# Other addresses and another order for some of the matmuls of a two-layer decoder trunk: Up weights shifted in 16-byte steps, tokens read backwards, two tiles taken in turn

## The chip, the cores and the metric

One NeuronCore of one Trainium2 chip runs the whole forward pass for one sequence of 256 tokens. The metric is device time in microseconds (us) of one execution. Within the core, TensorE (PE) multiplies matrices from the on-chip memory SBUF into the accumulators of PSUM; VectorE (DVE) and ScalarE (ACT) do everything that is elementwise; GpSimd (POOL) does little here; SyncE (SP) issues nearly all transfers from the chip's main memory. The engines run on their own and wait for each other by semaphores. In a row of the profile, L169 is line 169 of the kernel, and PEld is the loading of a matmul's stationary operand, which overlaps the matmul before.

## The reference

The model width is 1024, there are 16 heads of 64, and the inner width of the channel mixer is 2816. Cut to what matters:

```python
x = x + short_conv_mixer(rms_norm(x, a_norm[0]), ...)         # layer 0
x = x + conv_glu_ffn(rms_norm(x, f_norm[0]), ...)
k_blk, v_blk, k_mean = shared_kv(x, kv_norm, w_k, w_v)         # layer 1
x = x + moba_attention(rms_norm(x, b_norm[0]), ...)
x = x + conv_glu_ffn(rms_norm(x, f_norm[1]), ...)
return rms_norm(x, final_norm)

def conv_glu_ffn(h, w_up, conv_w, conv_b, w_down):
    u = causal_dwconv(h @ w_up, conv_w) + conv_b               # 1024 -> 2 x 2816
    g, v = jnp.split(u, 2, axis=-1)
    return (jax.nn.silu(g) * v) @ w_down                       # 2816 -> 1024
```

All of it is in float32.

## The kernel before

**Three products for one.** Each operand of a large matmul is split into a high part (rounded to the type fp32r) and a low part (what is left, in fp32r too). A product of two such numbers is taken as high x high + high x low + low x high, so one tile product is three matmuls into one accumulator. `mm3` (lines 168 to 171) issues them: line 169 is weight-high with x-high, line 170 weight-high with x-low, line 171 weight-low with x-high. In the profile the parts are called hiB and loB (1 MB units of weights, 2048 floats per partition), hiS and loS (512 KB units), xh and xl (normed activations), sh and sl (hidden activations), oh and ol (attention output).

**Units.** Weights come in units, each loaded by SP into one of three raw buffers, rounded by ACT into hi (line 91) and subtracted by DVE into lo (line 97). `Unit.buffer` makes the hi and lo tiles: 64 floats longer than the unit, of which the unit takes a slice that begins `at_byte` bytes in. Up units had `at_byte` 0, most units of V 128, the Down units of layer 1 192.

**The channel mixer.** `ffn` (line 517) runs twice, for layer 0 and layer 1, over 22 Up units. For unit i, `up_step` takes 8 slices k of the width and, for each, two tiles of 128 weight columns (one of the gate half, one of the value half): 8 x 2 x 3 = 48 matmuls, with a tile of 128 x 128 weights as the stationary operand and one row of 256 tokens of xh or xl as the moving one. Both tiles accumulate in one PSUM bank, each in its half. Then DVE and ACT do scale, convolution and gate (`conv`, `gate`; lines 525, 532, 397, 543, 549, 394), and the Down unit of three steps earlier follows on PE with 24 matmuls. In layer 0 (`down_bank`) the weights are stationary and the tokens move; in layer 1 (`token_bank`) the tokens are stationary and the weights move.

**Order.** The schedule is written by hand: the program text sets the order on each engine. Within `conv`, DVE splits the low part of the next B unit, and ACT then the high part of one after it; within `gate` the same is done for S units. The load of a raw buffer is issued on SP when the low part has been taken from the unit that held it.

**Addresses.** The allocator puts hiB0 at byte 42560 of a partition, loB0 at 51008, and the other hi and lo tiles of both sizes likewise at 64 bytes past a multiple of 128. The tiles of xh and xl begin 64 past a multiple of 128 too; their class `Rows` puts the eight rows of tokens (1024 bytes each) 1216 bytes in, that is at a multiple of 128, and a second copy of row 0, `again`, 128 bytes in, that is at 64 past a multiple of 128. Units 2 and 6 of each `ffn` use the copy for k = 0. `Heads` places the rows of oh and ol at several offsets: rows 0 and 3 are at 64 past a multiple of 128, the others at a multiple. So nearly all matmuls of the kernel have the moving operand at 0 and the stationary one at 64 modulo 128 bytes, or the reverse where tokens are stationary; a few have both at 64.

Of the kernel before, what the change touches and what calls it, by code (L numbers as in the profile page):

```python
# [19 lines left out]
KT = D // 128  # L20
NH = 16
FF = 2816
FJ = FF // 128
# [5 lines left out]
BIG = 2 * KT * 128  # L29
# [13 lines left out]
def yoco_kernel(ctx: ExitStack, tc: tile.TileContext, t: dict, out: bass.AP):  # L43
    nc = tc.nc
    V, A, G, PE = nc.vector, nc.scalar, nc.gpsimd, nc.tensor
# [56 lines left out]
    def hi(tag, part=0, parts=1):  # L102

        n = ptr[tag][0]
        if n < len(by_tag[tag]) and (by_tag[tag][n].prev is None or by_tag[tag][n].prev.used):
            by_tag[tag][n].split_hi(part, parts)
            ptr[tag][0] += part == parts - 1

    def lo(tag, part=0, parts=1):

        n = ptr[tag][1]
        if n < len(by_tag[tag]) and by_tag[tag][n].hi is not None:
            by_tag[tag][n].split_lo(part, parts)
            if part == parts - 1:
                ptr[tag][1] += 1
                if n + RAW_BUFS[tag] < len(by_tag[tag]):
                    by_tag[tag][n + RAW_BUFS[tag]].load()
# [6 lines left out]
            MO += [Unit(t["w_mo"][i], SMALL) for i in ((0, 1) if j == 3 else (j - 2,))]  # L124
    MO += [Unit(t["w_mo"][j], SMALL) for j in (KT - 2, KT - 1)]
    UP, DN = [None, None], [None, None]
    UP[0] = [Unit(t["w_up"][0, i], BIG) for i in range(FJ)]
    DN[0] = [Unit(t["w_dn"][0, i], SMALL) for i in range(FJ)]
    heads = [("v", 0), ("v", 1), ("v", 2)] + [("q", j) for j in range(KT)] + [("v", 3)]
    WH = {k: Unit(t["w_v" if k[0] == "v" else "w_qk"][k[1]], BIG, (0, 1), 128 if k[0] == "v" and k[1] else 0)  # L130
# [12 lines left out]
    first = const.tile([128, 1], F32, name="first")  # L143
# [20 lines left out]
    def par(c, k=0):  # L164
        return pk[:, c + k:c + k + 1]


    def mm3(o, wh, wl, xh, xl, start, stop):
        PE.matmul(o, wh, xh, start=start, stop=False, skip_group_check=True)  # L169
        PE.matmul(o, wh, xl, start=False, stop=False, skip_group_check=True)  # L170
        PE.matmul(o, wl, xh, start=False, stop=stop, skip_group_check=True)  # L171

    def up_step(u, o, xh, xl, m, ks=range(KT), first=0, again=False):

        assert u.lo is not None
        wh, wl = u.v(u.hi, m), u.v(u.lo, m)
        for k in ks:
            h, lw = (xh.again, xl.again) if again and k == 0 else (xh[:, k, :], xl[:, k, :])
            for i in range(m):
                mm3(o[:, i, :], wh[:, k, i, :], wl[:, k, i, :], h, lw,  # L180
                    start=(k == first and i == 0), stop=(k == KT - 1))
        u.used = ks[-1] == KT - 1

# [52 lines left out]
    def up_bank():  # L236
        return psum.tile([128, 2, S], F32, name="up", bufs=3)
# [36 lines left out]
    def parts_tiles():  # L274
        return Rows("xh"), Rows("xl")
# [28 lines left out]
    def boundary(acc, x, gain, order=same, again=True):  # L304

        xh, xl = parts_tiles()
        sq = square_tile()
        for q in range(5):
            if q < 4:
                V.tensor_add(x[:, 2 * q:2 * q + 2, :], acc[q], x[:, 2 * q:2 * q + 2, :])  # L310
                scaled_hi(x, gain, (2 * q, 2 * q + 1), xh, order)
            if q:
                scaled_lo(x, gain, (2 * q - 2, 2 * q - 1), xh, xl, order)
                squares(x, sq, q - 1)
        sum_squares(sq, 0)
        lo("B", 0, 2)
        if not again:
            lo("B", 1, 2)
        sum_squares(sq, 1, order)
        if again:  # L320
            lo("B", 1, 2)
            tile_0_again(xh, xl)
        return xh, xl, sq
# [72 lines left out]
    def tap(o, u, w, back):  # L396
        V.scalar_tensor_tensor(o[:, back:], u[:, :S - back], w, o[:, back:], op0=OP.mult, op1=OP.add)  # L397
# [6 lines left out]
    xh, xl = parts_tiles()  # L404
# [23 lines left out]
    def mixer_a(j, fill=None):  # L428

        w = [par(P_CONV, 3 * j + n) for n in range(3)]  # L430
        m = tmp.tile([128, 2, S], F32, name="u", bufs=2)
        V.tensor_mul(m[:, 1, :], mc[j][:, 0, :], rr[:, 1, :])
        V.tensor_mul(m[:, 0, :], mc[j][:, 1, :], m[:, 1, :])
        o = tmp.tile([128, 2, S], F32, name="cv", bufs=2)
        A.activation(o[:, 0, :], m[:, 0, :], AF.Identity, scale=w[2])
        hi("B")
        if fill:
            lo(fill)
        tap(o[:, 0, :], m[:, 0, :], w[1], 1)
        tap(o[:, 0, :], m[:, 0, :], w[0], 2)  # L440
        V.tensor_mul(o[:, 1, :], o[:, 0, :], rr[:, 0, :])
        return o[:, 1, :]
# [33 lines left out]
    for i in range(2):  # L476
        o = mixer_a(i, "B")
# [8 lines left out]
    o = mixer_a(3, "B")  # L486
# [7 lines left out]
    for j in range(4, KT):  # L494
        mc[j] = up_bank()
        up_step(MC[j], mc[j], xh, xl, 2)
        o = mixer_a(j, "S")
# [13 lines left out]
    xh, xl, sq = boundary(acc, xT, P_FN)  # L511
# [5 lines left out]
    def ffn(layer, xh, xl, sq, bank=down_bank, between=None):  # L517
        ub, hd, low = {}, {}, {}
        up, dn = UP[layer], DN[layer]

        def conv(j, last=False):
            c0 = 2 * FJ * layer + j
            cw = [[par(P_FCW, 3 * (c0 + half * FJ) + n) for n in range(3)] for half in range(2)]
            u = tmp.tile([128, 2, S], F32, name="u", bufs=2)
            V.tensor_mul(u, ub[j], rr[:, 0:1, :].to_broadcast([128, 2, S]))  # L525
            if j:
                low[j - 1]()
            if not last:
                lo("B")
            o = tmp.tile([128, 2, S], F32, name="cv", bufs=2)  # L530
            for half in range(2):
                A.activation(o[:, half, :], u[:, half, :], AF.Identity, scale=cw[half][2],  # L532
                             bias=par(P_FCB, c0 + half * FJ))
            hi("B")
            for back in (1, 2):
                for half in range(2):
                    tap(o[:, half, :], u[:, half, :], cw[half][2 - back], back)
            return o

        def gate(j, o, last=False):  # L540
            sl = tmp.tile([128, S], F32, name="sl", tag="sc", bufs=4)
            hi("S", 0, 1 + last)
            A.activation(sl, o[:, 0, :], AF.Silu)
            if last:
                hi("S", 1, 2)
            else:
                lo("S")
            hid = tmp.tile([128, S], F32, name="hid", tag="sc", bufs=4)
            V.tensor_mul(hid, sl, o[:, 1, :])  # L549
            hd[j], zh, low[j] = split_act(hid, S, 64 if layer == 0 else 128)  # L550
            zh()
            if last:
                lo("S", 0, 2)
                low[j]()
                lo("S", 1, 2)

        acc = None
        for i in range(FJ):
            if i != 2:
                ub[i] = up_bank()  # L560
            if i == 1:
                n = 4 if layer else 3
                up_step(up[1], ub[1], xh, xl, 2, range(1, n), first=1)
                _, dg = rstd_cols(sq)
                lo("S")
                A.activation(first, ones[:, 0:1], AF.Silu)
                up_step(up[1], ub[1], xh, xl, 2, (*range(n, 7), 0, 7), first=1, again=True)
                n = 2 if layer else 1
                ub[2] = up_bank()
                up_step(up[2], ub[2], xh, xl, 2, range(1, n + 1), first=1)  # L570
                rr = rstd_rows(dg)
                gate(0, conv(0))
            else:
                again = i in (2, 6)
                ks = (*range(n + 1 if i == 2 else 1, 7), 0, 7) if again else range(8)
                up_step(up[i], ub[i], xh, xl, 2, ks, first=int(again), again=again)
            last = i == FJ - 1
            if i:
                o = conv(i, last)
                if not last:  # L580
                    gate(i, o)
            if between and 5 <= i < 21:
                between(i - 5)
            if i >= LAG:
                if i == LAG:
                    acc = [acc_bank() for _ in range(4)]
                    if bank is token_bank:
                        acc.append(psum.tile([128, 2, S], F32, name="misc", bufs=1))
                down_step(dn[i - LAG], acc, hd[i - LAG], first=(i == LAG), bank=bank)
            if last:  # L590
                gate(i, o, True)
            elif i == FJ - 2:
                hi("S")
                lo("S")
            if i == 0:
                hi("B")
        if bank is token_bank:
            token_last(dn[FJ - 3:], acc, [hd[j] for j in range(FJ - 3, FJ)])
        else:
            down_step(dn[FJ - 3], acc, hd[FJ - 3])  # L600
            down_last(dn[FJ - 2:], acc, [hd[FJ - 2], hd[FJ - 1]])
        return acc
# [293 lines left out]
    xh, xl, sq = boundary(acc, xT, P_FN + KT)  # L896
# [19 lines left out]
    w = tmp.tile([128, 16], F32, name="nl", bufs=1)  # L916
# [101 lines left out]
```

## Time and profile before

| | |
|---|---|
| time, median of 2 runs | 568.63 us (568.47 to 568.80) |
| span of the profiled execution, first to last instruction | 566.6 us |
| PE busy, share of the span, matmuls | 558.4 us, 99%, 4908 |
| DVE busy | 472.9 us, 83% |
| ACT busy | 341.7 us, 60% |
| DMA share of 16 engines, main queue | 52.9% |
| mean granted TensorE clock | 0.997 |

The profiled execution has a span of 566.6 us; the median of the runs is 2.0 us more, and that difference lies around the span (start and end of the execution), where the profile shows no instruction of the engines.

How to read it: a matmul's time in a row (276 ns) is that of one from start to end, but they are pipelined, and the next starts long before the first ends. So the pace of PE is read from windows: the length of a stretch divided by the matmuls that start in it. In a row of the view by windows, the number behind "x" counts every instruction that touches the stretch, so also the two or three that began before it.

### The profile page before, as it was taken

To read this page: it belongs to the slowest core of one execution; us is meant where nothing else is said; L and a number is where in the kernel's file an instruction comes from. 1 tells how busy PE (TensorE), PEld (TensorE's weight loads), DVE (VectorE), ACT (ScalarE), POOL (GpSimd) and SP (SyncE) were. 2 spreads that over 40 slices of the span, in tenths; PEclk is the share of its full clock that TensorE was granted. 3 is DMA by queue.
4 is the path that set the end of the run, shared out by engine and by line. 5 is a ranking of instruction groups with operands and counts; after the bars stand their busy time and mean duration, and the time that the engine had idled before them with its cause. 6 is when DMAs were issued, how large, how long until landed. Compare 5 with 4: busy or idle time off the path is not lost.

```text
span 566.6 us, 11823 instructions
## 1 busy us (share of the span) xinstructions
PE 558.4 (99%) x4908; PEld 554.1 (98%) x4908; DVE 472.9 (83%) x817; ACT 341.7 (60%) x525; POOL 10.4 (2%) x32
## 2 busy tenths in 40 slices
PE   8999999999999999999999999999999999999995
PEld 8999999999999999999999999999999999999995
DVE  5998869899877787787897999858999888889876
ACT  7765437567654665466756777656676556546534
POOL 0400000000000000000000000000000000000001
PEclk9999999999999999999999999999999999999998
DMA  8986583447556545655265565644656554563211
GB/s 294 387 300 220 181 299 120 149 152 243 193 197 224 186 160 213 223 175 197 75 214 168 202 206 216 195 178 150 223 186 223 223 193 159 208 222 117 72 38 75
DMA packets 24181, 108.48 MB, mean 191 GB/s; under 512 B 2736, under 2 KB 5440, under 8 KB 16192
## 3 DMA queue, kind: packets, MB, share of 16 engines
q1 hardware_dynamic: 23840, 107.43, 52.9%
q8 instruction: 38, 0.62, 0.4%
q10 hardware_dynamic: 288, 0.30, 0.1%
q14 instruction: 15, 0.12, 0.1%
HBM read 106.65 MB, written 1.07 MB: 190 GB/s over the span
## 4 chain that ended last, share of the span: by engine, by line
PE 97%; DMA 1%; ACT 1%; issue 0%; DVE 0%; SPq 0%; POOLq 0%; POOL 0%; ACTq 0%
PE up L171 20%; PE up L169 20%; PE up L170 20%; PE acc L169 7%; PE acc L171 7%; PE acc L170 7%; PE acc L203 3%; PE acc L200 3%; PE acc L202 3%; PE up L757 1%; PE acc L627 1%; PE acc L629 1%; PE acc L630 1%; DMA xres<-xT 1%; PE acc L682 1%; PE misc L203 0%
## 5 line engine op out<-in xcount | busy, mean ns | idle before, releaser
L169 PE MATMUL up<-xh,hiB 128*128 128x256 f32 x944 | 261.4, 277 | 0.8 <-ACT hiB L91 0.8
L171 PE MATMUL up<-xh,loB 128*128 128x256 f32 x944 | 261.1, 277 | 0.3 <-DVE loB L97 0.2
L170 PE MATMUL up<-xl,hiB 128*128 128x256 f32 x944 | 260.8, 276 | 0.0
L169 PEld LDWEIGHTS up<-xh,hiB 128*128 128x128 f32 x944 | 177.2, 188 | 1.5 <-ACT hiB L91 1.0
L171 PEld LDWEIGHTS up<-xh,loB 128*128 128x128 f32 x944 | 177.2, 188 | 0.7 <-DVE loB L97 0.7
L170 PEld LDWEIGHTS up<-xl,hiB 128*128 128x128 f32 x944 | 177.3, 188 | 0.0
L97 DVE TENSOR_TENSOR loB<-rawB,hiB 128x2048 fp32r<-128x2048 f32 (+2 forms) x76 | 147.8, 1948 | 3.7 <-ACT hiB L91 3.5
L91 ACT ACTIVATE hiB<-rawB 128x2048 fp32r<-128x2048 f32 (+1 forms) x73 | 123.6, 1697 | 15.2 <-PE up L170 7.0
L532 ACT ACTIVATE cv<-u,pk 128x256 f32<-128x256 f32 x88 | 48.2, 595 | 69.3 <-DVE u L525 69.3
L97 DVE TENSOR_TENSOR loS<-rawS,hiS 128x1024 fp32r<-128x1024 f32 (+2 forms) x73 | 83.5, 1147 | 6.4 <-ACT hiS L91 6.0
L397 DVE SCALAR_TENSOR_TENSOR cv<-u,pk,cv 128x255 f32<-128x255 f32 x192 | 81.4, 479 | 2.7 <-ACT cv L532 1.7
L91 ACT ACTIVATE hiS<-rawS 128x1024 fp32r<-128x1024 f32 (+2 forms) x73 | 72.0, 987 | 8.9 <-PE acc L170 5.3
L525 DVE TENSOR_TENSOR u<-up,rr 128x512 f32<-128x512 f32 x44 | 30.3, 688 | 44.9 <-PE up L171 43.0
L171 PE MATMUL acc<-sh,loS 128*128 128x256 f32 x240 | 66.2, 276 | 0.0
L169 PE MATMUL acc<-sh,hiS 128*128 128x256 f32 x240 | 66.2, 276 | 0.0
L170 PE MATMUL acc<-sl,hiS 128*128 128x256 f32 x240 | 66.2, 276 | 0.0
L394 ACT ACTIVATE sh<-hid 128x256 fp32r<-128x256 f32 x52 | 21.7, 417 | 58.5 <-DVE hid L549 53.7
L171 PEld LDWEIGHTS acc<-sh,loS 128*128 128x128 f32 x240 | 45.1, 188 | 0.0
L169 PEld LDWEIGHTS acc<-sh,hiS 128*128 128x128 f32 x240 | 45.1, 188 | 0.0
L170 PEld LDWEIGHTS acc<-sl,hiS 128*128 128x128 f32 x240 | 45.0, 188 | 0.0
L200 PE MATMUL acc<-hiS,sh 128*128 128x256 f32 x154 | 42.5, 276 | 0.0
L202 PE MATMUL acc<-loS,sh 128*128 128x256 f32 x154 | 42.5, 276 | 0.0
(180 smaller groups left out, 780.3 us busy)
## 6 DMA issues: line engine op xcount, KB each, us to landing
rawB<-w_up SPq DMA_DIRECT2D x44, 1024.0 KB, 4.7
rawS<-w_dn SPq DMA_DIRECT2D x44, 512.0 KB, 3.4
rawB<-w_qk SPq DMA_DIRECT2D x8, 1024.0 KB, 4.8
rawB<-w_mc SPq DMA_DIRECT2D x6, 1024.0 KB, 8.1
rawS<-w_mo SPq DMA_DIRECT2D x8, 512.0 KB, 5.1
rawB<-w_v SPq DMA_DIRECT2D x4, 1024.0 KB, 4.7
rawS<-w_o SPq DMA_DIRECT2D x8, 512.0 KB, 4.0
rawS<-w_mb SPq DMA_DIRECT2D x7, 512.0 KB, 5.7
```

Of the source, the lines that this page charges most:

```text
L91: A.activation(self.hi[:, c], self.raw[:, c], AF.Copy)
L97: V.tensor_sub(self.lo[:, c], self.raw[:, c], f32(self.hi[:, c]))
L169: PE.matmul(o, wh, xh, start=start, stop=False, skip_group_check=True)
L170: PE.matmul(o, wh, xl, start=False, stop=False, skip_group_check=True)
L171: PE.matmul(o, wl, xh, start=False, stop=stop, skip_group_check=True)
L200: PE.matmul(o, hh[:, tok], u.hi[:, f], start=(first and (apart or d.start == 0)), stop=False, skip_group_check=True)
L202: PE.matmul(o, hh[:, tok], u.lo[:, f], start=False, stop=False, skip_group_check=True)
L203: PE.matmul(o, hl[:, tok], u.hi[:, f], start=False, stop=last, skip_group_check=True)
L394: return (h, lw), lambda: A.activation(h, src, AF.Copy), lambda: V.tensor_sub(lw, src, f32(h))
L397: V.scalar_tensor_tensor(o[:, back:], u[:, :S - back], w, o[:, back:], op0=OP.mult, op1=OP.add)
L525: V.tensor_mul(u, ub[j], rr[:, 0:1, :].to_broadcast([128, 2, S]))
L532: A.activation(o[:, half, :], u[:, half, :], AF.Identity, scale=cw[half][2], bias=par(P_FCB, c0 + half * FJ))
```

## The change

Three edits, all of which touch only matmuls of the two `ffn` calls and the buffers they read:

1. **Offsets.** Up unit i of layer 0 gets `at_byte` = 16 x max(0, i - 5) modulo 256: units 0 to 5 and 21 stay at 0, unit 6 gets 16, unit 7 gets 32, and so on to unit 20 with 240. ACT and DVE write the parts there, and PE loads its stationary tiles from there.
2. **Backwards.** In layer 1, units 9, 13, 17 and 21 pass `rev` to `up_step`. The row of 256 tokens is then read from its last to its first element, and the accumulator is written from its last to its first element as well, so each result lands where it did.
3. **In turn.** In layer 1, units 7, 11, 15 and 19 take their two tiles in turn: for each k, high x high of tile 0 and of tile 1, then high x low of both, then low x high of both.

The third edit moves instructions on PE. Below is the start of unit 7 of layer 1 as the program before has it; misc is the last accumulator of the Down unit ahead of it, hiB1_5410 and loB1_5505 are the two parts of the unit's weights, up_5659 its PSUM bank.

```order
L202 MATMUL misc_5326<-loS1_5420,sh_5319 128x256
L203 MATMUL misc_5326<-hiS1_5417,sl_5320 128x256
L169 MATMUL up_5659<-xh_4952,hiB1_5410 128x256 [waits PE_49]
L170 MATMUL up_5659<-xl_4953,hiB1_5410 128x256
L171 MATMUL up_5659<-xh_4952,loB1_5505 128x256 [waits DVE_49]
L169 MATMUL up_5659<-xh_4952,hiB1_5410 128x256
```

And the same place in the changed program, where line 182 issues the matmuls of such a unit:

```order
L208 MATMUL misc_5326<-loS1_5420,sh_5319 128x256
L209 MATMUL misc_5326<-hiS1_5417,sl_5320 128x256
L182 MATMUL up_5659<-xh_4952,hiB1_5410 128x256 [waits PE_49]
L182 MATMUL up_5659<-xh_4952,hiB1_5410 128x256
L182 MATMUL up_5659<-xl_4953,hiB1_5410 128x256 x2
L182 MATMUL up_5659<-xh_4952,loB1_5505 128x256 [waits DVE_49]
L182 MATMUL up_5659<-xh_4952,loB1_5505 128x256
L182 MATMUL up_5659<-xh_4952,hiB1_5410 128x256 x2
```

The first matmul that needs the low part, and so waits for DVE, is now the fifth of the unit and no longer the third. The end of the same unit before, with the Down unit behind it:

```order
L170 MATMUL up_5659<-xl_4953,hiB1_5410 128x256
L171 MATMUL up_5659<-xh_4952,loB1_5505 128x256
L200 MATMUL acc_5322<-hiS2_5519,sh_5426 128x256 [waits Activation_49]
L202 MATMUL acc_5322<-loS2_5522,sh_5426 128x256 [waits DVE_49]
L203 MATMUL acc_5322<-hiS2_5519,sl_5427 128x256
```

And after:

```order
L182 MATMUL up_5659<-xl_4953,hiB1_5410 128x256 x2
L182 MATMUL up_5659<-xh_4952,loB1_5505 128x256 x2
L206 MATMUL acc_5322<-hiS2_5519,sh_5426 128x256 [waits Activation_49]
L208 MATMUL acc_5322<-loS2_5522,sh_5426 128x256 [waits DVE_49]
L209 MATMUL acc_5322<-hiS2_5519,sl_5427 128x256
```

The unit still ends with the low part, and nothing else has moved; DVE, ACT, POOL and SP have the same rows in the same order throughout. The first two edits leave every row in its place and change addresses and steps alone. The diff:

```diff
-    UP[0] = [Unit(t["w_up"][0, i], BIG) for i in range(FJ)]
+    UP[0] = [Unit(t["w_up"][0, i], BIG, at=16 * max(0, i - 5) % 256) for i in range(FJ)]
...
-    def up_step(u, o, xh, xl, m, ks=range(KT), first=0, again=False):
+    def up_step(u, o, xh, xl, m, ks=range(KT), first=0, again=False, order=lambda a: a, turns=False):
 
         assert u.lo is not None
         wh, wl = u.v(u.hi, m), u.v(u.lo, m)
         for k in ks:
             h, lw = (xh.again, xl.again) if again and k == 0 else (xh[:, k, :], xl[:, k, :])
+            if turns:
+                for n, (w, x) in enumerate(((wh, h), (wh, lw), (wl, h))):
+                    for i in range(m):
+                        PE.matmul(o[:, i, :], w[:, k, i, :], x, start=(k == first and n == 0 and i == 0),
+                                  stop=(k == KT - 1 and n == 2), skip_group_check=True)
+                continue
             for i in range(m):
-                mm3(o[:, i, :], wh[:, k, i, :], wl[:, k, i, :], h, lw,
+                mm3(order(o[:, i, :]), wh[:, k, i, :], wl[:, k, i, :], order(h), order(lw),
                     start=(k == first and i == 0), stop=(k == KT - 1))
...
-                up_step(up[i], ub[i], xh, xl, 2, ks, first=int(again), again=again)
+                up_step(up[i], ub[i], xh, xl, 2, ks, first=int(again), again=again,
+                        order=rev if layer and i > 6 and i % 4 == 1 else same,
+                        turns=layer and i > 6 and i % 4 == 3)
```

`rev` is `a[..., ::-1]`, `same` returns its argument.

## The prediction

> **What bounds the kernel now.** I read the page first: the busy times and the chain of work that ended last.
>
> ```profile
> PE 558.4 (99%) x4908; PEld 554.1 (98%) x4908; DVE 472.9 (83%) x817; ACT 341.7 (60%) x525; POOL 10.4 (2%) x32
> PE 97%; DMA 1%; ACT 1%; issue 0%; DVE 0%; SPq 0%; POOLq 0%; POOL 0%; ACTq 0%
> ```
>
> PE is the chain: 97% of the way from the end back to the start is matmul after matmul. Next, the view of waits for PE alone, because a PE that is busy 99% could still be held up a little at each unit.
>
> ```profile
> PE misc L142 <- POOL ones L138: 1.0, 1, 1.0
> PE up L169 <- ACT hiB L91: 0.8, 1, 0.8
> PE up L171 <- DVE loB L97: 0.2, 1, 0.2
> ```
>
> That is the whole list: 2.0 us of waiting in 566.6. No transfer, no split and no gate holds PE. So only the pace of the matmuls can move the time, and the third view is the one by windows: the length of a stretch against the matmuls that the program starts in it.
>
> ```profile
> core 0: us, PE busy (x) PEld busy (x) DVE busy (x) ACT busy (x) POOL busy (x), PEclk, DMA share, GB/s
> 141.81:264.21 122.40, 122.40 (x1082) 122.40 (x1081) 94.44 (x136) 70.22 (x91) 0.00 (x0) 1.00 0.54 197
> 144.53:149.97 5.44, 5.44 (x50) 5.44 (x49) 3.76 (x7) 2.83 (x4) 0.00 (x0) 1.00 0.65 233
> 136.33:141.81 5.48, 5.48 (x50) 5.48 (x49) 4.81 (x7) 3.87 (x5) 0.00 (x0) 1.00 0.71 247
> 355.26:358.10 2.84, 2.84 (x27) 2.84 (x26) 2.05 (x7) 1.42 (x2) 0.00 (x0) 1.00 0.75 314
> 358.10:360.82 2.72, 2.72 (x27) 2.72 (x25) 2.63 (x7) 1.06 (x1) 0.00 (x0) 1.00 0.04 9
> 275.10:280.54 5.44, 5.44 (x51) 5.44 (x49) 5.44 (x10) 5.33 (x13) 0.00 (x0) 1.00 0.00 0
> 280.54:283.25 2.71, 2.71 (x26) 2.71 (x25) 2.44 (x5) 2.51 (x3) 0.00 (x0) 1.00 0.61 178
> 429.79:549.47 119.68, 119.68 (x1059) 119.68 (x1057) 102.52 (x148) 66.06 (x88) 0.00 (x0) 1.00 0.44 161
> ```
>
> The first row is layer 0 from the Down matmuls behind unit 6 to the end of unit 21: 1080 matmuls in 122.40 us, 113.3 ns each, at a granted clock of 1.00. Unit 7 alone (second row) is 48 in 5.44, again 113.3. The last row, units 7 to 21 of layer 1 with the Down units between them, is 1056 in 119.68: 113.3. This is a floor that PE holds without a gap, and each ns more on a matmul goes straight into the span.
>
> The other rows show what can lift a matmul off the floor. The step 355.26 to 358.10 is the first of the output projection, 24 matmuls whose moving rows (row 0 of oh and ol) lie at 64 modulo 128, as their stationary weights do: 2.84 us, 118.3 ns each. The next 24, with moving rows at 0, take 2.72: 113.3. Unit 6 of layer 0, where 6 of 48 matmuls use the row copy that lies at 64, takes 5.48 instead of 5.44. So a clash of the two addresses modulo 128 costs about 5.0 ns a matmul; unit 6 gives 0.04 us / 6 = 6.7. V's first step (275.10 to 280.54; moving at 64, stationary at 0) is on the floor at 5.44: what counts is that the two differ, not which is where. And the row at 280.54 shows a slower pace without a clash: 23 intervals in 2.71 us, 117.8 ns (moving at 64, stationary at 0).
>
> **Edit 1, offsets.** 15 units x 48 = 720 matmuls of layer 0, moving rows at 0, stationary tiles at 64 + 16n modulo 128, n = 1 to 15. For n = 4 and 12 both are at 0: the full 5.0 ns. For n = 8 they differ by 64, as now: nothing. The other twelve have no row. Their lower end is 0, their upper end the clash, and I take the share of the way from one to the other: 1/4, 1/2, 3/4 for n = 1, 2, 3, then back down, since a tile of weights that starts a quarter of 64 bytes in lies for a quarter of its length where the moving row is. These shares sum to 8 full units: 8 x 48 x 5.0 = **1.9 us**. The ends: nothing, and 720 x 6.7 = 4.8 us. A gain I leave out of the sum: two opposite placements (0 with 64, 64 with 0) give the same 113.3, so the floor does not look like one of addresses.
>
> [...]
>
> ACT and DVE now write these parts 16 to 240 bytes further in. For DVE the rows show no price: the convolution's taps, which start 4 or 8 bytes into a row, take as long as the same operation that starts at its beginning.
>
> ```profile
> L397 DVE SCALAR_TENSOR_TENSOR cv<-u,pk,cv 128x255 f32<-128x255 f32 x96 | 42.8, 479 | 2.4 <-ACT cv L532 1.7 <-ACT cv L435 0.6
> L287 DVE SCALAR_TENSOR_TENSOR xl<-xres,pk,xh 128x256 fp32r<-128x256 f32 x40 | 17.2, 481 | 6.3 <-ACT xh L283 6.3
> 175.59 2.29 DVE L97 TENSOR_TENSOR loB<-rawB,hiB 128x2048 fp32r<-128x2048 f32 x1
> 176.38 1.91 ACT L91 ACTIVATE hiB<-rawB 128x2048 fp32r<-128x2048 f32 x1
> 177.18 0.28 PE L169 MATMUL up<-xh,hiB 128*128 128x256 f32 x1
> 185.34 0.28 PE L169 MATMUL up<-xh,hiB 128*128 128x256 f32 x1
> ```
>
> For ACT there is no such row, so cover must do: the low part that ends at 177.88 came too late for the unit that starts at 177.18 and is used at 185.34 at the earliest, 7.4 us later. ACT is busy 70.22 of 122.40 us; a doubled 1.91 us in each period of 8.16 would make that 57 + 23 = 80%, still under PE. Zero, then; if ACT took three times as long, the split would need more than its period leaves, and each unit would run late by the rest.
>
> **Edit 2, backwards.** 4 x 48 = 192 matmuls. No matmul of this trace reads or writes with step -1. ACT does, at the norm ahead of V: 8 of these 40 read their row from the end.
>
> ```profile
> L283 ACT ACTIVATE xh<-xres,pk x40: 491/493/511, 4.2 to 382.4; 128x256 fp32r<-128x256 f32 x40
> L364 ACT ACTIVATE rr<-misc 128x256 f32<-128x256 f32 x5 | 1.8, 382 | 8.0 <-PE misc L361 7.9
> ```
>
> Shortest, median and longest are 491, 493 and 511 ns: direction is free there, and one of the five reads of PSUM in the second row runs backwards too, in a mean of 382. For PE this is only a neighbour. But the address moves: the reading now begins in the last 64 bytes of the row, at 64 modulo 128, where the stationary tile (offset 0, so 64) begins as well. I charge the clash: 192 x 5.0 = **1.0 us**. The lower end is 0; the upper end is half pace, one more 113.3 ns each, 21.8 us, a rival below, because the nearest rows, on another engine, show no such step.
>
> **Edit 3, in turn.** Also 192 matmuls. Each passage in the new order is already in the old one: to the other tile's weights with the same x (line 171 to 169 within one k), to other weights, to the other x, to the other half of the bank. All run at the floor in the rows above, so **0**. The upper end is the slower pace without a clash: 192 x 4.5 = 0.9 us. The wait for the low part comes two matmuls later in the unit; as PE waits 0.2 us for loB in the whole span, that gains nothing.
>
> Nothing else waits on these edits: where a unit takes 0.2 us longer, the gate behind it starts that much later and has until the Down unit three steps on. Sum, against the profiled execution: 566.6 + 1.9 + 1.0 + 0 = 569.5 us of span, and with the 2.0 us around it, against the median of 568.63: 568.6 + 2.9 = **571.5 us**.
>
> **The rivals.** *Backwards at half pace.* If reading or accumulating from the end runs at half pace, each of the 192 takes 226.6 ns: 568.6 + 1.9 + 21.8 = 592.3 us, slower by 4%. For it: no matmul row shows this step, and PE takes its 256 columns in 113 ns where ACT needs 493, so ACT's rows say little of a reader four times as fast. Against it: neighbours in a row stay neighbours. It decides the verdict from about 50 ns more per matmul (11.4 - 1.9 = 9.5 us over 192). [...]
>
> *No address costs anything here.* The 118.3 of the output projection comes from something else at that place (it follows a change of kernel stage), and step -1 is free: 568.6 us, no change. [...] Against it: unit 6 of layer 0, in the middle of an even stretch, is late too.
>
> *The slower pace stays.* A shifted unit throws PE into the 117.8 ns of the row at 280.54, and it keeps it through the rest of the channel mixer: from unit 6 on 1128 matmuls in layer 0, and from unit 7 on 1056 in layer 1, each 4.5 ns more: 9.8 us, 578.4 us. Against it: after unit 6 the first row is back on 113.3.
>
> *A gain.* If some offset frees PE of part of the floor, 720 x some 4 ns would give about 565.7 us. Nothing in the rows speaks for it.
>
> **How the numbers follow.** The forecast of 571.5 has 0.66; its own range goes from 568.6 to 575.3 (4.8 + 1.0 + 0.9). No cost at all has 0.10, the lasting slower pace 0.05, half pace backwards 0.17, a gain 0.02. The likeliest case gives the time. The range 568.0 to 579.0 holds the first three, 0.81. A measurement of this kernel can tell about 2% from no change, here 11.4 us: below 557.3 or above 580.0. Slower is the half pace alone, 0.17; faster would need more than any case here gives, 0.01; within 2% the rest, 0.82.
>
> **What would show it.** By windows of one unit in the profile after: unit 13 of layer 0 (n = 8) 5.44 us, units 9 and 17 (n = 4, 12) 5.68, the others between; units 7, 11, 15 and 19 of layer 1 5.44; units 9, 13, 17 and 21 of layer 1 5.68, or 10.9 under the main rival. A wait of PE for hiB or loB of more than 0.2 us would contradict the cover. The prediction is wrong if backward units leave the pace of their neighbours by more than a clash, or if an offset costs more than 6.7 ns a matmul.

## The result, and the profile after

The changed kernel takes 573.95 us (median of 2 runs, 573.78 to 574.12) against 568.63 (568.47 to 568.80): a ratio of 1.0095, 95% interval 1.0066 to 1.0124, which is less than the 2% that count as a change here, and on the slow side. The profiled execution has a span of 572.3 us, 5.7 more than before.

The first view is the page of the kernel after: busy times, and the chain that ended last.

```profile
PE 564.0 (99%) x4908; PEld 559.6 (98%) x4908; DVE 472.8 (83%) x817; ACT 341.7 (60%) x525; POOL 10.4 (2%) x32
PE 97%; DMA 1%; ACT 1%; SPq 0%; issue 0%; DVE 0%; POOLq 0%; POOL 0%; ACTq 0%
```

The busy time of PE has grown by 5.6 us with the same 4908 matmuls, DVE and ACT are where they were. The view of PE's waits, after, in the columns "total us, times, longest":

```profile
PE misc L142 <- POOL ones L138: 1.0, 1, 1.0
PE up L169 <- ACT hiB L91: 0.7, 1, 0.7
PE up L171 <- DVE loB L97: 0.4, 2, 0.2
```

Still about 2 us in all. So the time came as slower matmuls, not as waiting, and windows show where. Kernel after, columns "window: length, PE busy (instructions touched), granted clock, DMA share, GB/s"; a unit has 48 matmuls (5.44 us on the floor of 113.3 ns), a Down unit 24 (2.72 us):

```profile
136.96:263.59 126.63, 126.63 (x1082) 1.00 0.52 191
136.96:142.66 5.70, 5.70 (x50) 1.00 0.70 255
142.66:145.49 2.83, 2.83 (x26) 1.00 0.53 203
...
153.85:159.60 5.75, 5.75 (x50) 1.00 0.68 251
162.34:168.03 5.69, 5.69 (x50) 1.00 0.66 238
...
187.74:193.40 5.66, 5.66 (x50) 1.00 0.70 248
193.40:196.23 2.83, 2.83 (x26) 1.00 0.17 65
196.23:201.88 5.65, 5.65 (x50) 1.00 0.68 248
...
204.61:210.20 5.59, 5.59 (x50) 1.00 0.66 248
...
434.60:440.04 5.44, 5.44 (x50) 1.00 0.58 197
450.92:456.58 5.66, 5.66 (x51) 1.00 0.67 237
```

The first row is layer 0 from the start of unit 6 to the end of the Down unit behind unit 20, 15 Up and 15 Down units. The same stretch before:

```profile
136.33:258.77 122.44, 122.44 (x1082) 1.00 0.54 198
```

That is 4.19 us more, all of it in edit 1's units and the Down units between them. The rows below it are unit 6 (offset 16) and the Down unit behind it, unit 8 (48), unit 9 (64), unit 12 (112), the Down unit behind it, unit 13 (128), and unit 14 (144). The Down units have their weights where they were, yet two of them take 2.83 us: 117.8 ns a matmul, the slower pace that the prediction found in a row of V. The last two rows are layer 1: unit 7, whose tiles take turns, on the floor, and unit 9, backwards, 0.22 us above it.

One more difference lies ahead of every edit. The chain in order of time (start us, duration, what) has the four matmuls of the first norm here after:

```profile
19.88 0.34 PE misc L348 x4
```

and here before:

```profile
19.25 0.34 PE misc L342 x4
```

0.63 us of the 5.7 are there already at 20 us, in the first loads and the first matmuls, which no edit touches. About 0.2 us of it is the slower pace again. The same 48 matmuls ahead of that norm, before and after:

```profile
12.97:18.41 5.44, 5.44 (x51) 1.00 1.03 406
...
13.35:19.01 5.66, 5.66 (x51) 1.00 1.04 416
```

The balance: 4.2 in layer 0, 4 x 0.22 = 0.9 in the backward units of layer 1, 0.6 at the start, 5.7 in all.

### The profile page after: what moved, and what is told of

Same layout as the page of the kernel before. It is cut to its first block, busy times and chain, and to the rows that moved or that the text cites. A ratio compares the mean times of both kernels' runs of the same rounds, so it can differ in the third digit from the quotient of the medians.

```text
span 572.3 us, 11823 instructions
## 1 busy us (share of the span) xinstructions
PE 564.0 (99%) x4908; PEld 559.6 (98%) x4908; DVE 472.8 (83%) x817; ACT 341.7 (60%) x525; POOL 10.4 (2%) x32
## 4 chain that ended last, share of the span: by engine, by line
PE 97%; DMA 1%; ACT 1%; SPq 0%; issue 0%; DVE 0%; POOLq 0%; POOL 0%; ACTq 0%
PE up L169 18%; PE up L171 18%; PE up L170 18%; PE acc L169 7%; PE acc L170 7%; PE acc L171 7%; PE up L182 4%; PE acc L206 3%; PE acc L209 3%; PE acc L208 3%; PE up L765 1%; DMA xres<-xT 1%; PE acc L635 1%; PE acc L638 1%; PE acc L637 1%; PE acc L690 1%
## 5 line engine op out<-in xcount | busy, mean ns | idle before, releaser
L169 PE MATMUL up<-xh,hiB 128*128 128x256 f32 x880 | 245.3, 279 | 0.7 <-ACT hiB L91 0.7
L171 PE MATMUL up<-xh,loB 128*128 128x256 f32 x880 | 245.1, 279 | 0.6 <-DVE loB L97 0.4
L170 PE MATMUL up<-xl,hiB 128*128 128x256 f32 x880 | 244.5, 278 | 0.0
L169 PEld LDWEIGHTS up<-xh,hiB 128*128 128x128 f32 x880 | 165.4, 188 | 1.3 <-ACT hiB L91 0.9
L171 PEld LDWEIGHTS up<-xh,loB 128*128 128x128 f32 x880 | 165.4, 188 | 1.2 <-DVE loB L97 1.2
L170 PEld LDWEIGHTS up<-xl,hiB 128*128 128x128 f32 x880 | 165.5, 188 | 0.0
```

## Experiments

All ratios and differences are against the kernel before, run on the same chip in the same job (568.67, 568.98 or 568.76 us in the three jobs). Where no interval is given, there is one execution, and its windows are what counts.

### Each edit alone

Edit 1 alone:

```diff
-    UP[0] = [Unit(t["w_up"][0, i], BIG) for i in range(FJ)]
+    UP[0] = [Unit(t["w_up"][0, i], BIG, at=16 * max(0, i - 5) % 256) for i in range(FJ)]
```

> Edit 1 alone. In the profile after, units 6 to 20 of layer 0 and the Down units between them carry 4.2 us of the 5.7 us by which the span grew. If the three edits add up, this kernel takes 568.6 + 4.2 = 572.8 us and its layer 0 repeats the windows of the changed kernel (5.60 to 5.76 us per shifted unit). Rival: the edits act on each other or the 4.2 us is a chance of that one execution; then the time lies away from 572.8 by more than 1 us.

Measured: 572.79 us, ratio 1.0075 (1.006 to 1.009), 4.1 us more. The window of layer 0 in this kernel:

```profile
136.82:263.46 126.64, 126.64 (x1083) 1.00 0.52 191
```

The same length within 0.01 us as with all three edits: the cost belongs to the addresses and repeats.

Edit 2 alone:

```diff
+                        order=rev if layer and i > 6 and i % 4 == 1 else same)
```

> Edit 2 alone. By the clash of addresses the four backward units take 5.65 us each instead of 5.44: 568.6 + 0.9 = 569.5 us. Rival: the backward units cost more or less when layer 0 is undisturbed; then the windows of units 9, 13, 17 and 21 differ from 5.65 by more than 0.02 us.

Measured: 569.53 us, ratio 1.0019 (1.001 to 1.0028), 0.9 us more; each of the four units like this one:

```profile
446.56:452.21 5.65, 5.65 (x50) 1.00 0.70 244
```

Edit 3 alone:

```diff
+                        turns=layer and i > 6 and i % 4 == 3)
```

> Edit 3 alone. Expected at the floor: 5.44 us in units 7, 11, 15 and 19 of layer 1 and 568.6 us in all. Rival: the order has a price that the other edits hid; then more than 5.44.

Measured: 568.45 us, ratio 1.000 (0.999 to 1.001), units at 5.44. Taking turns cost nothing. The three add up to 4.1 + 0.9 - 0.2 = 4.8 us, where the whole change measured 5.3, with an interval of 3.8 to 7.1 (its ratio times 568.63).

### Why backwards costs: is it the start, or the direction?

My reason for edit 2 was that reading from the end moves the first address to 64 modulo 128, where the stationary tile begins. Then weights moved by 64 bytes would take the cost away.

```diff
+    UP[1] = [Unit(t["w_up"][1, i], BIG, (0, 1) if i < 2 else (0, 1, 2), 64 if i > 6 and i % 4 == 1 else 0)
+             for i in range(FJ)]
...
+                        order=rev if layer and i > 6 and i % 4 == 1 else same)
```

> Edit 2 with the weights of the four backward units moved by 64 bytes, so that reading from the end of the row (64 modulo 128) meets a stationary tile at 0 modulo 128. Theory of the clash: the price goes, 5.44 us per unit and 568.6 us. Rival, reading or accumulating backwards costs something by itself: 5.65 us per unit stays, 569.5 us.

Measured: 569.98 us, ratio 1.0027 (1.0016 to 1.0037). Unit 9, backwards with its weights moved, and unit 10, untouched:

```profile
446.20:451.95 5.75, 5.75 (x50) 1.00 0.70 246
454.67:460.11 5.44, 5.44 (x50) 1.00 0.70 240
```

Not the floor but 5.75 us, more than without the move. The clash of starts is not the reason. Two more kernels asked what is. In the first, all eight odd units from 7 on in layer 1 read and write backwards, with their weights at 0, 16, 32 and so on to 112 bytes:

```diff
+    UP[1] = [Unit(t["w_up"][1, i], BIG, (0, 1) if i < 2 else (0, 1, 2), 8 * (i - 7) if i > 6 and i % 2 else 0)
...
+                        order=rev if layer and i > 6 and i % 2 else same)
```

> The kernel before, with eight backward units in layer 1 (7, 9, ... 21) whose weights start 0, 16, ... 112 bytes in; the even units stay as they were. Theory of opposite directions: a moving row read downwards and a stationary tile read upwards meet wherever they start, so all eight take 5.6 to 5.76 us (0: 5.65, 64: 5.75, as seen). Rival, the clash is one of where they start: at least one of the eight offsets takes 5.44 us.

Measured: 570.92 us. The units at offsets 0, 16 and 64, at the last two with the end of another instruction in the count:

```profile
430.25:435.90 5.65, 5.65 (x50) 1.00 0.59 194
446.80:452.46 5.66, 5.66 (x51) 1.00 0.70 242
...
496.50:502.25 5.75, 5.75 (x51) 1.00 0.67 244
```

No offset of the eight brings the floor back: 4.4 ns to 6.5 ns a matmul each. In the second, the two halves of "backwards" are taken apart: units 9 and 13 only read from the end, units 17 and 21 only write from the end. Each of these four units so delivers its tokens in reverse, and the output is not the reference's; the work is the same.

```diff
-                mm3(o[:, i, :], wh[:, k, i, :], wl[:, k, i, :], h, lw,
+                mm3(back(o[:, i, :]), wh[:, k, i, :], wl[:, k, i, :], order(h), order(lw),
...
+                        order=rev if layer and i in (9, 13) else same,
+                        back=rev if layer and i in (17, 21) else same)
```

> In layer 1, units 9 and 13 only read their tokens backwards and units 17 and 21 only write their accumulators backwards, so these four units deliver their tokens in reversed order, which changes what follows from them but not its work. If the price of a backward unit is a clash of the two reads, units 9 and 13 take 5.65 us and 17 and 21 take 5.44. Rival, writing backwards costs: 17 and 21 take more than 5.44.

Measured: 569.32 us. Units 9, 17 and 21 (13 is like 9):

```profile
446.57:452.22 5.65, 5.65 (x50) 1.00 0.66 238
...
512.30:517.74 5.44, 5.44 (x50) 1.00 0.66 227
544.94:550.38 5.44, 5.44 (x50) 1.00 0.01 3
```

The whole price is in the reading, 0.21 us in 48 matmuls or 4.4 ns each; writing PSUM from the end costs nothing. The 117.8 ns of a backward unit are the slower pace to the tenth, and the untouched Down unit behind is nearly back on the floor (2.73 us). Whether reading from the end has a price of its own, or puts PE on the slower pace for as long as it lasts, these runs do not separate.

### What an offset costs, away from its neighbours

In the change, shifted units follow one another with only Down units between. Here every second unit is shifted, so that each has untouched ones on both sides: offsets 16 to 128 in units 7, 9, ... 21 of layer 0, 144 to 240 in units 7 to 19 of layer 1 (unit 21 is back at 0).

```diff
+    UP[0] = [Unit(t["w_up"][0, i], BIG, at=8 * (i - 5) if i > 6 and i % 2 else 0) for i in range(FJ)]
...
+                  (128 + 8 * (i - 5)) % 256 if i > 6 and i % 2 else 0) for i in range(FJ)]
```

> The kernel before, with one shifted Up unit at a time: in layer 0 units 7, 9, ... 21 start 16, 32, ... 128 bytes in, in layer 1 they start 144, 160, ... 240 and 0 bytes in; the even units stay at 0. Theory of clash and carry: a unit pays only while its two reads meet, and a slower pace of 117.8 ns lasts on into what follows; so 128 alone (layer 0, unit 21) costs nothing, 5.44 us, since nothing slow comes before it, 64 and 192 cost 5.65 to 5.76, and an even unit behind a shifted one takes 5.44 or, where the pace is carried, up to 5.65. Rival, position modulo 256: 128 costs 5.65 alone as well. Rival, linear shares: 16 and 112 cost 5.50, 32 and 96 5.56.

Measured: 574.18 us. Units 7 (16), 8 (untouched) and 9 (32) of layer 0; then from unit 19 (112) on, with the Down unit, unit 20 (untouched), the Down unit and unit 21 (128):

```profile
144.78:150.49 5.71, 5.71 (x51) 1.00 0.64 233
153.21:158.65 5.44, 5.44 (x50) 1.00 0.67 241
161.38:167.14 5.76, 5.76 (x51) 1.00 0.69 240
...
244.55:250.21 5.66, 5.66 (x50) 1.00 0.66 238
250.21:253.04 2.83, 2.83 (x26) 1.00 0.22 85
253.04:258.69 5.65, 5.65 (x50) 1.00 0.64 250
258.69:261.53 2.84, 2.84 (x27) 1.00 0.14 56
261.53:267.18 5.65, 5.65 (x51) 1.00 0.71 245
```

Two things are in these rows. An offset of 16 costs as much as one of 64 (5.5 and 5.2 ns a matmul, in the table below), where I had charged a quarter: there is no share; weights off the grid of 64, against tokens on it, cost 3.2 to 6.7 ns. And behind the unit at 112, an untouched unit and two untouched Down units run at 117.7 to 118.3 ns: what the shifted unit set off outlives it. Worked out from the starts of the matmuls in all such windows, in ns per matmul above 113.3:

| offset | 16 | 32 | 48 | 64 | 80 | 96 | 112 | 128 | 144 | 160 | 176 | 192 | 208 | 224 | 240 |
|---|---|---|---|---|---|---|---|---|---|---|---|---|---|---|---|
| after (layer 0) | 5.6 | 4.1 | 6.5 | 5.2 | 6.4 | 6.5 | 4.7 | 4.4 | 3.2 | 3.2 | 4.0 | 6.6 | 5.1 | 4.9 | 4.4 |
| every second unit | 5.5 | 6.7 | 6.5 | 5.2 | 6.4 | 6.5 | 4.7 | 4.4 | 3.2 | 3.2 | 4.0 | 6.6 | 5.1 | 4.9 | 4.4 |

The last three of both rows stand inside a stretch of the slower pace that the unit at 192 left, and say nothing of their own. The rows agree within 0.1, but for 32: in the change the Down unit ahead of it is already slow (2.83 us), and it takes 4.1 instead of 6.7. The number at 128 is in both rows the carried pace, not the offset's own, as the next experiment shows.

### Is it modulo 128, and is it the two operands against each other?

Clean multiples first: all units of layer 0 from 7 on at 64 (as the moving rows modulo 128), those of layer 1 at 128 (64 apart from them, as before).

```diff
+    UP[0] = [Unit(t["w_up"][0, i], BIG, at=64 if i > 6 else 0) for i in range(FJ)]
...
+    UP[1] = [Unit(t["w_up"][1, i], BIG, (0, 1) if i < 2 else (0, 1, 2), 128 if i > 6 else 0) for i in range(FJ)]
```

> Up units 7 to 21 start 64 bytes in (layer 0) and 128 bytes in (layer 1). Theory of the clash: every such unit of layer 0 takes 5.65 to 5.76 us (stationary and moving both at 0 modulo 128), every one of layer 1 takes 5.44. Rival, position modulo 256: layer 1 takes 5.65 too.

Measured: 572.15 us. A unit of layer 0 and one of layer 1:

```profile
144.30:149.99 5.69, 5.69 (x51) 1.00 0.67 240
433.55:438.99 5.44, 5.44 (x51) 1.00 0.53 179
```

At 64 each unit costs 5.2 ns a matmul, at 128 nothing: on multiples of 64 the rule that the prediction read from the output projection holds here. Modulo 128 is not the whole of it, though: 16 and 144 stand alike modulo 128 and cost 5.5 and 3.2 ns in the table above, and 64 and 192, which both clash, 5.2 and 6.6. The same matmul takes 118.5 ns instead of 113.3 when only the place of its weights is changed. How the place acts, no row shows.

Then both operands off the grid together: the weights of all units of layer 0 and the rows of tokens 16 bytes later. In layer 1 only the tokens move.

```diff
+    UP[0] = [Unit(t["w_up"][0, i], BIG, at=16) for i in range(FJ)]
...
-            self.rows = t[:, 48 + S:48 + S + KT * S].rearrange("p (k s) -> p k s", s=S)
+            self.rows = t[:, 52 + S:52 + S + KT * S].rearrange("p (k s) -> p k s", s=S)
```

> The rows of xh and xl and all Up weights of layer 0 start 16 bytes later; everything else stays. In layer 0 moving and stationary keep their relation, but neither begins on a multiple of 64 bytes. Theory of the clash (only the relation counts): the Up units of layer 0 stay on 5.44 us. Rival, a start off the 64-byte grid costs by itself: 5.6 us or more in each. In layer 1 the moving rows alone are 16 bytes late (16 against 64): about 5.65 us by either.

Measured: 581.07 us, 12.1 more. A unit of layer 0 and one of layer 1:

```profile
148.02:153.48 5.46, 5.46 (x51) 1.00 0.66 233
438.17:443.89 5.72, 5.72 (x50) 1.00 0.66 244
```

With both shifted a unit is 0.02 us from the floor; with tokens alone shifted it is 0.28 above it. So a start 16 bytes off the grid costs next to nothing by itself; the cost comes with where the two stand to each other. (Most of the 12.1 us are matmuls whose tokens moved and whose weights stayed: some 5 us in the Up units of layer 1, and others outside `ffn`; in the short-conv mixer of layer 0, 48 such matmuls take 5.72 too.)

### What is the slower pace, and what ends it?

In the kernel before, the copy of row 0 clashes in units 2 and 6, and also in unit 1 and a few products outside `ffn`. Unit 1 reads it soon after the four small matmuls of the norm at 101.4 us. In the kernel before, 18 matmuls between those four and the copy, and 30 behind the copy:

```profile
102.48:104.60 2.12, 2.12 (x21) 1.00 0.77 189
...
106.02:109.42 3.40, 3.40 (x32) 1.00 0.49 174
```

That is 117.8 ns ahead of the clash and 113.3 behind it. Was it the clash that brought PE back from the slower pace? Here the copy begins 64 bytes earlier, where it does not clash.

```diff
-            self.again = t[:, 32:32 + S]
+            self.again = t[:, 16:16 + S]
```

> The copy of row 0 that units 2 and 6 and a few others use starts 64 bytes earlier, at 0 modulo 128, and no longer meets the weights. If a clash only costs, each of its uses saves 0.05 us or more (some ten of them, 0.5 us). Rival: the slower pace of 117.8 ns that follows the norm (unit 1 of each channel mixer) ended before because the clash knocked PE out of it; without the clash it lasts, and units 2 to 5 take 5.65 us instead of 5.44, up to 2 us in all or more if it lasts through the mixer.

Measured: 572.72 us, 3.7 more, with these clashes gone. 48 matmuls of the short-conv mixer, 72 behind the small matmuls of the next norm (unit 1's reads of the copy among them), unit 3 of `ffn`, and the six matmuls of unit 6 that read the copy:

```profile
46.82:52.47 5.65, 5.65 (x51) 1.00 0.75 266
...
106.03:114.51 8.48, 8.48 (x74) 1.00 0.50 181
...
123.48:128.92 5.44, 5.44 (x50) 1.00 0.18 74
...
143.88:144.59 0.71, 0.71 (x9) 1.00 1.03 438
```

From the small matmuls of the norm at 20 us on (a wait of PE the profile does not show there), the whole mixer runs at 117.8 ns, and so do the matmuls behind the next norm, to 114.7 us, at the end of unit 2's reads of the copy; then the floor is back. So the pace of 117.8 is a state that lasts here, and longer with the clash gone: where the kernel before has the clash soon after the small matmuls of the norm at 101.4 us, it is back on the 113.3 at once. The expected gain of 0.5 us did not come; the rival came true, in the mixer more than in the units that it names. Two things speak against the clash as the whole story. Unit 2 left the slower pace at the copy without a clash, and in unit 6 the six matmuls of the copy still take 118 ns each, though they lie 64 apart: unit 6 takes 5.47 us where it took 5.48 before. So most of the 0.04 us that the prediction read there as the price of a clash is there without one. Whether a clash always ends the slower pace was asked next: one unit in each layer, unit 7, at 112 (the offset that left the slower pace behind it), and in unit 11 of layer 0 the clashing copy.

```diff
+    UP[0] = [Unit(t["w_up"][0, i], BIG, at=112 if i == 7 else 0) for i in range(FJ)]
...
+    UP[1] = [Unit(t["w_up"][1, i], BIG, (0, 1) if i < 2 else (0, 1, 2), 112 if i == 7 else 0) for i in range(FJ)]
...
-                again = i in (2, 6)
+                again = i in (2, 6) or layer == 0 and i == 11
```

> The kernel before with unit 7 of both layers 112 bytes in, the offset that left PE on the slower pace; in layer 0 unit 11 also reads the copy of row 0, whose six matmuls clash. Theory of the carried pace: in both layers unit 8 and what follows run at 117.8 ns (5.65 us per Up unit, 2.83 per Down unit) although nothing about them is changed; in layer 0 the clash in unit 11 ends it and unit 12 is back on 5.44; in layer 1 nothing ends it, so 14 Up and 14 Down units pay 0.21 and 0.11 us, 4.5 us in all. Rival, the pace dies out by itself: units 9 to 21 of layer 1 are on 5.44.

Measured: 578.62 us, 9.9 more, from 2 x 48 matmuls with another address. In layer 0 unit 7, the Down unit behind it, unit 11 with the clash, unit 12, and the four Down units at the end (96 matmuls, 10.88 on the floor); in layer 1 the last 95 matmuls of the kernel:

```profile
144.33:149.99 5.66, 5.66 (x50) 1.00 0.69 242
149.99:152.82 2.83, 2.83 (x26) 1.00 0.18 72
178.26:183.92 5.66, 5.66 (x50) 1.00 0.71 244
186.75:192.40 5.65, 5.65 (x50) 1.00 0.71 250
...
268.72:280.03 11.31, 11.31 (x98) 1.00 0.33 112
...
559.33:570.52 11.19, 11.19 (x98) 1.00 0.00 1
```

Everything behind unit 7 stays at 117.8 ns: in layer 0 for 138 us, through the clash of unit 11, the end of `ffn` and the start of V, until the norm's small matmuls at 288 us and the copy that V reads behind them, which clashes; in layer 1 to the end of the kernel. 138 us and the 130 us of layer 1, with 4.5 of every 117.8 ns too much, are 10.2 us; the 9.9 is against other executions of the kernel before, whose first 20 us differ by some tenths. The clash in unit 11 did not end it, so the part of the expectation that said so is wrong.

### Can the kernel before be improved by this?

Units 2 and 6 on the ordinary row 0, and rows 0 and 3 of oh and ol on multiples of 128, so that none of them clashes.

```diff
-                up_step(up[i], ub[i], xh, xl, 2, ks, first=int(again), again=again)
+                up_step(up[i], ub[i], xh, xl, 2, ks, first=int(again))
...
-            at = 48 + j * S + (48 if j == 3 else 64 if j > 3 else 0 if j else -16)
+            at = 48 + j * S + (64 if j > 2 else 0)
```

> The kernel before, with units 2 and 6 of each channel mixer on the ordinary row 0 and rows 0 and 3 of the attention output moved to multiples of 128 bytes, so 72 matmuls no longer clash. If a clash only costs: 4 units save 0.05 us and the output projection 0.3 us, about 568.2 us. Rival: the clash in the projection also ends the slower pace that follows a wait there; without it the pace lasts and the time is 568.7 us or more.

Measured: 568.36 us against 568.76, ratio 0.9996 (0.9987 to 1.0005): no difference. The first 24 matmuls of the output projection, and its last 120:

```profile
355.33:358.17 2.84, 2.84 (x27) 1.00 0.76 320
...
366.22:379.94 13.72, 13.72 (x122) 1.00 0.63 222
```

The first row is as slow as before without its clash; the last 120 gain 0.14 us. Unit 6 of layer 0, on the ordinary row, takes 5.44. So in the prediction's 2.84 us row the slower pace would have done as well as the clash, and it was no clean proof of the rule; `grid_64` is.

## Why the prediction was right, and where it was not

**The bound: right.** PE waits some 2 us in all, before as after, and what the matmuls grew by went into the span: PE is busy 5.6 us longer, and the span is 5.7 longer. The offsets cost ACT and DVE nothing, as the rows of both engines after show; the same groups took a mean of 2284 and 1909 ns before:

```profile
L97 DVE TENSOR_TENSOR loB<-rawB,hiB 128x2048 fp32r<-128x2048 f32 x58 | 132.5, 2284 | 3.0 <-ACT hiB L91 2.9
...
L91 ACT ACTIVATE hiB<-rawB 128x2048 fp32r<-128x2048 f32 x61 | 116.4, 1908 | 13.8 <-PE up L170 7.0 <-PE acc L638 3.3 <-issue 2.3
```

**Edit 1: right sign, half the size.** The step that failed is "the share of the way from one to the other": 1.9 us in the sum, 4.2 measured, inside its range of 0 to 4.8 only because the upper end charged every matmul 6.7 ns. Two things were missing. The quarter steps do not exist: the Up units alone cost 3.5 us, and each offset off the grid of 64 that was measured clear of a carried pace costs 3.2 to 6.7 ns a matmul, in no order of distance (16 costs more than 144, though the two are the same modulo 128). And a cost can reach past its unit: five Down units behind units 6, 12, 17, 18 and 19 took 2.83 us for 2.72, 0.65 us with smaller remainders in others. Unit 13, charged with nothing, shows the second: its own offset of 128 is free (`grid_64`), but it came in on the pace that unit 12 left, and took 5.65. Charging the full clash of 5.0 ns to all 14 offsets but 128 would have given 3.4 us and nearly the Up units' sum. That price of 5.0 was itself luck: neither row that it came from was a clean clash (`fewer_clashes`, `copy_apart`), but the clean one of `grid_64` gives 5.2.

**Edit 2: right amount by luck, wrong reason.** 1.0 us forecast, 0.9 measured. "I charge the clash" fell twice: with the weights moved out of the way a backward unit took 5.75 us, and in the scan no offset reached the floor. The cost sits in reading the moving operand from the end. Whether the direction costs by itself, or meets the weights' reads in another way at every one of the eight offsets, or is the slower pace, is open. ACT's rows, which read both ways alike (491 to 511 ns), told nothing of PE here.

**Edit 3: right**, 0 forecast and 0 measured, alone and with the others.

**The rivals.** *Half pace backwards* was an assumption that no run had shown, and it fell: 5.65 us a unit, not 10.9. Units 17 and 21 of `read_or_write`, which only write PSUM from the end, ran at 5.44. *No address costs anything* fell with `grid_64`: 5.69 us a unit at 64, 5.44 at 128. *The slower pace stays* is a real mechanism that I gave 0.05: the change shows it for single Down units and unit 13, and one unit at 112 in each layer had it for almost the rest of the kernel, 9.9 us, near the 9.8 of the rival, which counted the two channel mixers alone. The change itself escapes most of it: its slow stretches end with the units at 32, 128 and 240, and those of `isolated` with the units at 128 and 240. In `carry` no shifted unit followed, and the pace stayed. Why these units end it is not shown. The argument I held against it, that the pace was back on the floor after unit 6 before, said nothing of other offsets.

**The sum.** A span of 572.3 us came against 569.5: 1.6 us more in the Up units, 0.65 carried into Down units, 0.1 less in edit 2, and 0.6 in the first 20 us, which differ from one execution to another and belong to no edit.

## What to carry to other kernels

When PE is the bound and its matmuls run at an even pace, the place of one operand against the other in a partition can be worth what it was here, 3% to 6% of a matmul (3.2 to 6.7 ns of 113.3): keep the starts of moving and stationary tiles on multiples of 64 bytes and 64 apart modulo 128 (in these runs that was the floor of 113.3 ns in the Up and Down units wherever the slower pace had not set in; the six matmuls of the copy in `copy_apart`, at 118 ns, are the exception), and read the moving operand forwards (backwards cost 4.4 to 6.5 ns more); the order of tiles and the direction of PSUM writes were free here (5.44 us a unit). Price a disturbance by the windows of the untouched units behind it as well: in `carry` a unit that cost 0.2 us itself left a slower pace that cost about 5. An operation's freedom on one engine is not to be taken over to another without a row of that engine.

## What the runs showed of the hardware that was not expected

Matmuls of 128 x 256 in a stream, with a new stationary tile for each, had two steady paces in these runs, at the same granted clock of 1.00 and the same addresses: 113.3 and 117.8 ns. The second was entered behind a unit at 112 or 192 bytes, behind unit 6 of the change (16 bytes, and the copy), behind a norm's four small matmuls, or in the first 20 us, and lasted up to 138 us. No change of address is needed: the 48 matmuls from 13 to 19 us, the same in the kernel before and in eleven of the other kernels, ran at 113.3 ns in eight of these twelve executions and at 117.8 in four (after, `offsets_alone`, `backwards_scan`, `fewer_clashes`). It was seen to end with a clash behind a norm's small matmuls (before, 105 us; `carry`, 288 us), with a unit at 32, 128 or 240 bytes, or, in `copy_apart` at 114.7 us, with reads of the copy that did not clash; the norm's small matmuls alone (`copy_apart`, 105 us) and the clash on 6 matmuls in unit 11 of `carry` did not. What the two paces are, what moves PE between them, and why the offsets off the grid differ from 3.2 to 6.7 ns, stays open. Nearly all of the 9.9 us (1.7%) that `carry` took more are this state, and no wait in its profile shows it: PE waits 1.2 us there in all.
